# Eight instead of four column tiles of an MLP product by seven products, with a narrow first product

## The chip, the cores and the metric

The kernel runs on one core of one Trainium2 chip. The metric is device time in microseconds (us) of one execution. Three runs of the kernel before the change gave 1551.36, 1551.41 and 1552.81 us, median 1551.41. TensorE is called PE, VectorE DVE, ScalarE ACT; SP issues the loads.

## The reference

One decoder layer on 256 tokens with 2048 features: a mixer sub-layer (gated linear recurrence and windowed attention), then the MLP that the change touches, then a final RMSNorm. All operands are float32.

```python
h2 = _modulate(_rms_norm(x, norm2_g[l]), shift2, scale2)
ff = jnp.square(jax.nn.relu(jnp.einsum("bsd,df->bsf", h2, w_ff1[l])))
x = x + gate2[:, None, :] * jnp.einsum("bsf,fd->bsd", ff, w_ff2[l])
return _rms_norm(x, final_g)
```

`w_ff1` is 2048 x 8192, `w_ff2` 8192 x 2048. With tiles of 128, ff1 has 64 column tiles of 16 row tiles each, and ff2 16 column tiles of 64 row tiles.

## The kernel before

**Precision.** Each float32 operand is split into a rounded high part and the rest as a low part (`split` for activations, L165 to L167; for weights `w_round`, L178 on ACT, and `w_rest`, L183 on DVE). A product is high x high, high x low, low x high: three matmuls with 256 moving columns in the narrow form (`gemm`, L204 to L206), or one with 512 columns (high and low of the activations side by side) and one with 256 in the wide form (`gemm_wide`, L226 to L232). The wide form leaves two halves of a bank, which ACT copies (L236) and DVE adds (L237); where `join=False` the two halves are taken one after the other.

**Chunks.** The MLP runs in four chunks of 16 ff1 column tiles each. In a chunk, `ff1_unit(c, f)` computes one column tile of the first product (f from 0 to 15; called F below) and keeps its square; then `ff2_unit(c, f)` multiplies the 16 squares with the chunk's rows of one column tile of `w_ff2` and adds the result to the residual `x1[f]` on DVE (L1183). Each such unit reads 1 MB of weights.

**Seven products.** In chunks 1 to 3 the ff2 column tiles 0 to 3 are not computed one by one. A `sum_step` (called S below) takes two row tiles (p of 8 pairs) and four column tiles: as a 2 x 2 block product, with the token halves of the two squares against the four blocks of 128 x 256 weights, by Winograd's form of Strassen's scheme. It has seven block products instead of eight, each again three matmuls with 256 moving columns (L1017 to L1019), 21 in all, which add up over the eight steps in seven half banks. `token_sums` (L974 to L985) makes the four sums of the squares (L978 to L981 on DVE, L983 on ACT, L984 on DVE), `weight_sums` (L987 to L999) the four sums of the weights: it loads 2 x 256 KB in rows of 512 bytes (L991), L993 makes two differences, then one 1024-column part is rounded and split (L178, L183), L996 and L997 make the last two sums, and a 768-column part is rounded and split. At a chunk's end the seven results go out of PSUM to `yt` (L1025 on ACT in chunk 1, L1027 on DVE adding in chunks 2 and 3); after chunk 3 `join_sums` (L1038) combines them and `take_sums` turns them back with transposes (L1045) and adds them to `x1` (L1047).

**Order of the work.** `units` lists the units of the whole kernel. Before a unit runs, the weights of the two units after it are asked for (LOOK = 2). Loads go through four `raw` buffers of 1 MB, taken in turn, and rounded and split parts through four `wh` and four `wl` buffers, two of each per unit. Within this, the framework's scheduler orders each engine's instructions ahead of time by costs of its own; each engine then runs its list in that order. PSUM has two pools of four banks: `pg` for units, `pa` for the seven products and transposes. In chunks 1 to 3 an S stands after every second F, the last one after ff2's first unit.

Of the kernel before, what the change touches and what calls it, by code (L numbers as in the profile page):

```python
# [66 lines left out]
def hybrid_layer(ctx: ExitStack, tc: tile.TileContext, x, xt, wada, w_p, w_r, w_f, vec, lruw, relb,  # L67
# [932 lines left out]
    yt = scr[:, 0:7 * T].rearrange("p (a b) -> p a b", b=T)  # L1000

    def sum_step(c, p, u):
        def run(w):
            if p == 0:
                pq[0] = [bank([P, 2, T]) for _ in range(4)]
            hi, lo = ts.pop(p)
            fa, fb = ff[c, 2 * p], ff[c, 2 * p + 1]
# [4 lines left out]
            for n, ((xh, xl), i, o) in enumerate(prods):
# [3 lines left out]
                end = p == KT // 2 - 1 and (n % 2 == 1 or n == 6)  # L1016
                te.matmul(ps, lhsT=xh, rhs=wh[:, e], start=p == 0 and n % 2 == 0, stop=False)  # L1017
# [2 lines left out]
            if p == KT // 2 - 1:  # L1020
                for n in range(4):
                    m = min(2, 7 - 2 * n)
                    y, ps = yt[:, 2 * n:2 * n + m], pq[0][n][:, 0:m]
                    if c == SUMMED_FROM:
                        se.activation(y, ps, AF.Copy)  # L1025
                    else:
                        ve.tensor_tensor(out=y, in0=ps, in1=y, op=ALU.add)  # L1027
                if c == 3:
                    later(3.0, join_sums)
                    for f in range(0, SUMMED, 2):  # L1030
                        later(1.6, take_sums, f)
        add_unit(run, lambda: weight_sums(u, p), 1024)

    def join_sums():
        p1, p2, p3, p5, p7, p6, p4 = (yt[:, i] for i in range(7))
        for o, a, b, op in ((p6, p1, p6, ALU.add), (p2, p1, p2, ALU.add), (p7, p6, p7, ALU.add), (p3, p6, p3, ALU.add),
                            (p3, p3, p5, ALU.add), (p4, p7, p4, ALU.subtract), (p5, p7, p5, ALU.add)):
            ve.tensor_tensor(out=o, in0=a, in1=b, op=op)  # L1038

    def take_sums(f):  # L1040
        ca, cb = (yt[:, 2], yt[:, 3]) if f == 0 else (yt[:, 1], yt[:, 6])
        pt = bank([P, 2, T])
        for i in range(2):
            for b, y in enumerate((ca, cb)):
                te.transpose(pt[:, i, b * P:(b + 1) * P], y[:, i * P:(i + 1) * P], idt)  # L1045
# [165 lines left out]
    for f in range(16):  # L1211
        out_unit(f)
    for c in range(4):
        summed = SUMMED if c >= SUMMED_FROM else 0
        u2 = full[0] + 16
        for f in range(16):
            ff1_unit(c, f)
            if summed and f % 2 == 1 and f > 1:
# [133 lines left out]
```

## Time and profile before

| | |
|---|---|
| median of three runs | 1551.41 us |
| the profiled execution | 1553.18 us, its span 1551.4 us |
| PE busy | 1536.2 us, 99% |
| DVE busy | 1286.0 us, 83% |
| ACT busy | 932.7 us, 60% |
| chunk 1 | from 1010 us, ff2 from 1117 us |
| chunk 2 | from 1186 us, ff2 from 1293 us |
| chunk 3 | from 1362 us, ff2 from 1469 us, the end at 1551 us |

The span is the time from the first to the last instruction on the core. Views used: the page (busy times, the chain of waits that ended last), windows (busy times of each engine in a stretch), instructions of one line (their count, first and last start), and timelines: start, duration, engine, line, operation, output and inputs, count, and in brackets the engine's idle time before it with what ended it. A duration is longer by some 0.08 us than the distance from one start to the next, because DVE starts an instruction before the one ahead has quite ended; distances between starts are what add up.

### The profile page before, as it was taken

The numbers are of one execution on the slowest core, as the hardware profiler recorded it, in microseconds if no ns is written. First come the engines' busy times: TensorE is split into PE (matmuls) and PEld (weight loads), VectorE is DVE, ScalarE is ACT, GpSimd is POOL, SyncE is SP. The second block draws the span as 40 slices with busy tenths as digits, with TensorE's granted clock in tenths as the row PEclk, the third lists the DMA queues.
The fourth block names the chain that finished last, engine by engine and source line by source line (L and its number), as shares of the span: only waits on it lengthen the run. The fifth ranks groups of instructions, "written<-read, shape, count | busy, mean of one in ns | idle before, by whom it ended". The sixth has DMA issues, their size and how long they took to land.

```text
span 1551.4 us, 25653 instructions
## 1 busy us (share of the span) xinstructions
PE 1536.2 (99%) x10137; PEld 1394.9 (90%) x10137; DVE 1286.0 (83%) x2030; ACT 932.7 (60%) x1538; POOL 0.2 (0%) x4
## 2 busy tenths in 40 slices
PE   8999999999999999999999999999999999999998
PEld 7999999999988888888889988888988888888887
DVE  5899888889889899999898877888866887678885
ACT  5763456657998674444466763366744765357764
POOL 0000000000000000000000000000000000000000
PEclk9999999999999999999999999999999999999999
DMA  9899977564676759988877666865654556546551
GB/s 371 335 387 332 354 277 256 210 247 177 259 256 241 275 203 340 353 307 298 331 277 278 218 248 244 326 224 182 214 201 174 179 194 227 189 154 204 195 210 57
DMA packets 84744, 387.93 MB, mean 250 GB/s; under 512 B 7344, under 2 KB 36368, under 8 KB 44432
## 3 DMA queue, kind: packets, MB, share of 16 engines
q1 hardware_dynamic: 79632, 381.51, 67.4%
q10 hardware_dynamic: 4992, 4.79, 1.0%
q8 instruction: 79, 1.29, 0.3%
q14 instruction: 41, 0.34, 0.1%
HBM read 384.13 MB, written 2.15 MB: 249 GB/s over the span
## 4 chain that ended last, share of the span: by engine, by line
PE 95%; ACT 3%; DMA 1%; DVE 1%; issue 0%; SPq 0%; DVEq 0%; ACTq 0%
PE pg L230 41%; PE pg L229 20%; PE pg L204 6%; PE pg L205 6%; PE pg L206 6%; PE pg L232 1%; PE pa L1017 1%; PE pa L1019 1%; PE pa L1018 1%; PE pg L1066 1%; PE pg L1065 1%; PE pg L1064 1%; PE pg L370 1%; ACT wh L178 1%; DMA ra<-in_wada_dram 1%; PE pa L678 1%
## 5 line engine op out<-in xcount | busy, mean ns | idle before, releaser
L230 PE MATMUL pg<-k,wh 128*128 128x512 f32 x2832 | 981.6, 394 | 0.6 <-DVE k L167 0.6
L178 ACT ACTIVATE wh<-rw 128x1024 fp32r<-128x1024 f32 (+1 forms) x542 | 559.5, 1041 | 444.3 <-PE pg L230 297.9
L183 DVE TENSOR_TENSOR wl<-rw,wh 128x1024 fp32r<-128x1024 f32 (+1 forms) x542 | 643.8, 1200 | 157.9 <-ACT wh L178 152.3
L229 PE MATMUL pg<-k,wl 128*128 128x256 f32 x2655 | 743.5, 280 | 0.0
L230 PEld LDWEIGHTS pg<-k,wh 128*128 128x128 f32 x2832 | 521.4, 188 | 108.3 <-PE pg L230 0.9
L229 PEld LDWEIGHTS pg<-k,wl 128*128 128x128 f32 x2655 | 499.4, 188 | 8.3 <-ACT k L166 0.7
L204 PE MATMUL pg<-k,wh 128*128 128x256 f32 x878 | 249.3, 284 | 0.0
L205 PE MATMUL pg<-k,wh 128*128 128x256 f32 x878 | 245.4, 280 | 0.0
L206 PE MATMUL pg<-k,wl 128*128 128x256 f32 x878 | 245.1, 280 | 0.0
L283 DVE CUSTOM_DVE_ANT_0 ra<-ra,scr,vc 128x2048 f32<-128x2048 f32 x96 | 225.1, 2345 | 10.2 <-DMA ra<-in_wada_dram 7.8
L204 PEld LDWEIGHTS pg<-k,wh 128*128 128x128 f32 x878 | 165.0, 188 | 4.8 <-issue 4.6
L205 PEld LDWEIGHTS pg<-k,wh 128*128 128x128 f32 x878 | 165.0, 188 | 0.2
L206 PEld LDWEIGHTS pg<-k,wl 128*128 128x128 f32 x878 | 164.8, 188 | 0.0
L1183 DVE SCALAR_TENSOR_TENSOR k<-pg,mod,k 128x256 f32<-128x256 f32 x100 | 48.3, 483 | 18.6 <-PE pg L230 17.1
L236 ACT ACTIVATE t<-pg 128x256 f32<-128x256 f32 x127 | 46.6, 367 | 24.4 <-PE pg L230 24.4
L237 DVE TENSOR_TENSOR t<-pg,t 128x256 f32<-128x256 f32 x127 | 52.9, 417 | 2.9 <-ACT t L236 2.9
L232 PE MATMUL pg<-k,wl 128*128 128x256 f32 x177 | 49.4, 279 | 0.0
L686 ACT ACTIVATE t<-t,as 128x128 f32<-128x128 f32 x64 | 28.4, 445 | 22.3 <-DVE as L683 22.3
L1064 PE MATMUL pg<-z,wh 128*128 128x258 f32 x144 | 40.8, 284 | 0.0
L1065 PE MATMUL pg<-z,wh 128*128 128x256 f32 x144 | 40.8, 284 | 0.0
L1066 PE MATMUL pg<-z,wl 128*128 128x258 f32 x144 | 40.7, 283 | 0.0
L232 PEld LDWEIGHTS pg<-k,wl 128*128 128x128 f32 x177 | 33.2, 188 | 6.5
(217 smaller groups left out, 1354.5 us busy)
## 6 DMA issues: line engine op xcount, KB each, us to landing
rw<-in_w_f_dram SPq DMA_DIRECT2D x188, 1024.0 KB, 4.9
ra<-in_wada_dram SPq DMA_DIRECT2D x96, 1024.0 KB, 6.5
rw<-in_w_r_dram SPq DMA_DIRECT2D x30, 1024.0 KB, 5.0
rw<-in_w_p_dram SPq DMA_DIRECT2D x29, 960.0 KB, 7.0
rw<-in_w_f_dram SPq DMA_DIRECT2D x48, 256.0 KB, 3.5
bt<-ud ACTq DMA_DIRECT2D x8, 512.0 KB, 3.6
k<-in_w_p_dram SPq DMA_DIRECT2D x9, 256.0 KB, 11.3
lw<-in_lruw_dram SPq DMA_DIRECT2D x4, 512.0 KB, 5.7
```

The lines of the kernel that those rows point to most:

```text
L178: pin(se.activation(wh[:, :c], raw[:, o:o + c], AF.Copy))
L183: pin(ve.tensor_tensor(out=wl[:, :c], in0=raw[:, o:o + c], in1=wh[:, :c].bitcast(F32), op=ALU.subtract))
L204: pin(te.matmul(ps, lhsT=wh[:, w], rhs=hl[:, 0], start=k == 0, stop=False))
L205: pin(te.matmul(ps, lhsT=wh[:, w], rhs=hl[:, 1], start=False, stop=False))
L206: pin(te.matmul(ps, lhsT=wl[:, w], rhs=hl[:, 0], start=False, stop=k == n - 1))
L229: te.matmul(ps[:, 0], lhsT=wl[:, w], rhs=hl[:, 0], start=False, stop=False)
L230: te.matmul(ps, lhsT=wh[:, w], rhs=hl, start=k == 0, stop=k == n - 1)
L232: te.matmul(ps[:, 0], lhsT=wl[:, w], rhs=hl[:, 0], start=False, stop=False)
L283: pin(ve.tensor_tensor_reduce(out=raw, in0=raw, in1=scr, scale=1.0, scalar=vc[:, V_BADA + c:V_BADA + c + 1], op0=ALU.mult, op1=ALU.add, ac ...
L1064: te.matmul(ps, lhsT=wh[:, e], rhs=z[k][:, 0:258], start=k == 0, stop=False)
L1065: te.matmul(ps[:, 0:256], lhsT=wh[:, e], rhs=z[k][:, 258:514], start=False, stop=False)
L1066: te.matmul(ps, lhsT=wl[:, e], rhs=z[k][:, 0:258], start=False, stop=k == KT - 1)
```

## The change

`QUADS = 2`: in chunks 1 to 3 the column tiles 0 to 7 of ff2 go by seven products, as two quads of four. Each pair of row tiles p now has two steps, q = 0 and 1, with the same token sums and other weights. The 14 results need seven banks: the four of `pa` and three of `pg`. One `pg` bank is left for the units in between, so ff1 in chunks 1 to 3 and ff2's column tiles 8 to 11 use the narrow form in half a bank (`half_of`; two units share a bank, f below 4 has its own). ff1's result then goes to ACT's Relu straight from PSUM, and L236 and L237 fall away there. A step stands after every F from f = 3 on, and after ff2's units 8, 9 and 10. `yt` has seven tiles instead of a slice of one. At the end two joins and four takes are due instead of one and two.

```diff
-SUMMED, SUMMED_FROM = 4, 1
+SUMMED, SUMMED_FROM, QUADS = 4, 1, 2
@@ sums_out, sum_step
-    def sum_step(c, p, u):
+    def sums_out(c):
+        if not yt:
+            yt.extend(scr[:, i * 2 * T:(i + 1) * 2 * T].rearrange("p (a b) -> p a b", b=T) for i in range(4))
+            yt.extend(pair() for _ in range(7 * QUADS // 2 - 4))
+        for y, ps in zip(yt, pq.pop(0)):
+            if c == SUMMED_FROM:
+                se.activation(y, ps, AF.Copy)
+            else:
+                ve.tensor_tensor(out=y, in0=ps, in1=y, op=ALU.add)
+        if c == 3:
+            for q in range(QUADS):
+                later(1.2, join_sums, q)
+            for f in range(0, SUMMED * QUADS, 2):
+                later(1.2, take_sums, f)
+    def sum_step(c, p, u, q):
         def run(w):
-            if p == 0:
+            if p == 0 and q == 0:
                 pq[0] = [bank([P, 2, T]) for _ in range(4)]
-            hi, lo = ts.pop(p)
+                pq[0] += [pg.tile([P, 2, T], F32, tag="pg", name=nm("pg")) for _ in range(7 * QUADS // 2 - 4)]
+            hi, lo = ts[p]
...
-            for n, ((xh, xl), i, o) in enumerate(prods):
+            for n, ((xh, xl), i, o) in enumerate(prods, 7 * q):
@@ ff1_unit
-            gemm_wide(w, [zn[k] for k in range(KT)], out=t[:, 0])
-            se.activation(t[:, 0], t[:, 0], AF.Relu)
+            if c >= SUMMED_FROM:
+                se.activation(t[:, 0], gemm(w, 0, [zn[k] for k in range(KT)], half_of(f, f < 4)), AF.Relu)
+            else:
+                gemm_wide(w, [zn[k] for k in range(KT)], out=t[:, 0])
+                se.activation(t[:, 0], t[:, 0], AF.Relu)
@@ ff2_unit
+            if c >= SUMMED_FROM and f < SUMMED * QUADS + 4:
+                pss = [gemm(w, 0, acts, half_of(f))]
@@ the list of units
-        summed = SUMMED if c >= SUMMED_FROM else 0
+        summed = SUMMED * QUADS if c >= SUMMED_FROM else 0
+        steps = [(p, u2 + q * SUMMED, q) for p in range(KT // 2) for q in range(QUADS)] if summed else []
         for f in range(16):
             ff1_unit(c, f)
-            if summed and f % 2 == 1 and f > 1:
-                sum_step(c, f // 2 - 1, u2)
+            if f > 2 and steps:
+                sum_step(c, *steps.pop(0))
```

**DVE in ff1 of chunk 3.** Before: `wl` with 1024 columns from a raw that no L993 names is half of an F's weights (rw_14867, rw_14953), rw_14898 and rw_15044 are raws of two S steps. One S's second part (768 columns) and the next S's first difference (L993) stand in three F halves:

```order
L183 TENSOR_TENSOR wl_14871<-rw_14867,wh_14869 128x1024
L183 TENSOR_TENSOR wl_14875<-rw_14867,wh_14873 128x1024
L167 TENSOR_TENSOR k_14855<-t_14817,k_14855 128x256
L978 SCALAR_TENSOR_TENSOR t_14858<-t_14766,t_14817 128x128
L979 SCALAR_TENSOR_TENSOR t_14858<-t_14858,t_14766 128x128
L981 TENSOR_TENSOR t_14858<-t_14817,t_14858 128x128
L183 TENSOR_TENSOR wl_14904<-rw_14898,wh_14902 128x1024
L984 TENSOR_TENSOR ts_14864<-t_14858,ts_14863 128x512
L993 TENSOR_TENSOR rw_15044<-rw_15044 128x512
L183 TENSOR_TENSOR wl_14910<-rw_14898,wh_14908 128x768
```

There the raw for rw_15044 is the one that the F with rw_14867 gives back. Now, the same engine and stretch, from the last part of one S (rw_16025) to that of the next (rw_16125); F's raw is rw_16060, and the S after the next is rw_16233:

```order
L183 TENSOR_TENSOR wl_16037<-rw_16025,wh_16035 128x768
L984 TENSOR_TENSOR ts_16022<-t_16016,ts_16021 128x512
L996 TENSOR_TENSOR rw_16125<-rw_16125 128x256
L183 TENSOR_TENSOR wl_16064<-rw_16060,wh_16062 128x1024
L997 TENSOR_TENSOR rw_16125<-rw_16125 128x256
L993 TENSOR_TENSOR rw_16233<-rw_16233 128x512
L183 TENSOR_TENSOR wl_16068<-rw_16060,wh_16066 128x1024
L996 TENSOR_TENSOR rw_16233<-rw_16233 128x256
L183 TENSOR_TENSOR wl_16131<-rw_16125,wh_16129 128x1024
L167 TENSOR_TENSOR k_16122<-t_16070,k_16122 128x256
L183 TENSOR_TENSOR wl_16137<-rw_16125,wh_16135 128x768
```

With F and S in turn, the four raws make an S take over the raw of the S two before it: rw_16233 is loaded into the buffer of rw_16025, once the first row shown has read it. Five rows behind that row its first difference is due.

**The next step on DVE**, up to the last part of rw_16233; rw_16333 takes over the buffer of rw_16125, rw_16160 is the next F's:

```order
L997 TENSOR_TENSOR rw_16233<-rw_16233 128x256
L183 TENSOR_TENSOR wl_16164<-rw_16160,wh_16162 128x1024
L993 TENSOR_TENSOR rw_16333<-rw_16333 128x512
L183 TENSOR_TENSOR wl_16168<-rw_16160,wh_16166 128x1024
L978 SCALAR_TENSOR_TENSOR t_16224<-t_16070,t_16170 128x128
L980 TENSOR_TENSOR t_16224<-t_16070 128x128
L979 SCALAR_TENSOR_TENSOR t_16224<-t_16224,t_16070 128x128
L167 TENSOR_TENSOR k_16221<-t_16170,k_16221 128x256
L981 TENSOR_TENSOR t_16224<-t_16170,t_16224 128x128
L183 TENSOR_TENSOR wl_16239<-rw_16233,wh_16237 128x1024
L984 TENSOR_TENSOR ts_16230<-t_16224,ts_16229 128x512
L183 TENSOR_TENSOR wl_16245<-rw_16233,wh_16243 128x768
```

Here only two rows stand between L993 and the row that gives its buffer back, and the second half of the next F's weights (wl_16168) behind L993.

**PE near the end of chunk 3.** Before, the transposes of `take_sums` (L1045) stand inside an ff2 unit (pg_15665), more than one unit after the last S:

```order
L230 MATMUL pg_15665<-k_14508,wh_15536 128x512
L1045 MATMUL pa_15576<-idt,scr 128x128
L1045 MATMUL pa_15591<-idt,scr 128x128 x4
L229 MATMUL pg_15665<-k_14559,wl_15538 128x256
L230 MATMUL pg_15665<-k_14559,wh_15536 128x512
```

Now (L1056) half of them stand between ff2's units 11 and 12, one unit after the last S:

```order
L206 MATMUL pg_16890<-k_16637,wl_16888 128x256
L1056 MATMUL pa_16996<-idt,scr 128x128
L1056 MATMUL pa_17011<-idt,scr 128x128 x4
L1056 MATMUL pa_16996<-idt,scr 128x128 x3
L230 MATMUL pg_17129<-k_15174,wh_16946 128x512
```

What they turn comes from the joins on DVE (L1049), which stand there behind the weights of unit 12 (wl_16948, wl_16952) and three adds out of PSUM:

```order
L183 TENSOR_TENSOR wl_16948<-rw_16944,wh_16946 128x1024
L183 TENSOR_TENSOR wl_16952<-rw_16944,wh_16950 128x1024
L1010 TENSOR_TENSOR k_12765<-pg_15412,k_12765 128x512
L1010 TENSOR_TENSOR k_12766<-pg_15413,k_12766 128x512
L1010 TENSOR_TENSOR k_12767<-pg_15414,k_12767 128x512
L1049 TENSOR_TENSOR scr<-scr 128x256 x3
L1049 TENSOR_TENSOR k_12767<-scr,k_12767 128x256
L1049 TENSOR_TENSOR scr<-scr 128x256
```

The first join ends with the last row shown; the second has six more rows behind it, one of them after the first takes.

More of the change, by code (lines that the diff above doesn't have):

```diff
@@ L998, in weight_sums @@
         return parts + [w_rest(flat, 5 * T, 3 * T, w_round(flat, 5 * T, 3 * T))]
-    yt = scr[:, 0:7 * T].rearrange("p (a b) -> p a b", b=T)
-    def sum_step(c, p, u):
+    yt = []
+    def sums_out(c):
[13 more added lines that the diff above has]
+    def sum_step(c, p, u, q):
         def run(w):
-            if p == 0:
+            if p == 0 and q == 0:
                 pq[0] = [bank([P, 2, T]) for _ in range(4)]
-            hi, lo = ts.pop(p)
+                pq[0] += [pg.tile([P, 2, T], F32, tag="pg", name=nm("pg")) for _ in range(7 * QUADS // 2 - 4)]
+            hi, lo = ts[p]
             fa, fb = ff[c, 2 * p], ff[c, 2 * p + 1]
@@ L1015, in run @@
                 wh, wl = w[i]
-                end = p == KT // 2 - 1 and (n % 2 == 1 or n == 6)
+                end = p == KT // 2 - 1 and n % 2 == 1
                 te.matmul(ps, lhsT=xh, rhs=wh[:, e], start=p == 0 and n % 2 == 0, stop=False)
@@ L1019, in run, with joined, join_sums @@
                 te.matmul(ps, lhsT=xl, rhs=wh[:, e], start=False, stop=end)
[L1020 to L1031, printed above, removed]
+            if q == QUADS - 1:
+                ts.pop(p)
+                if p == KT // 2 - 1:
+                    sums_out(c)
         add_unit(run, lambda: weight_sums(u, p), 1024)
-    def join_sums():
-        p1, p2, p3, p5, p7, p6, p4 = (yt[:, i] for i in range(7))
+    def joined(q, i):
+        return yt[(7 * q + i) // 2][:, (7 * q + i) % 2]
+    def join_sums(q):
+        p1, p2, p3, p5, p7, p6, p4 = (joined(q, i) for i in range(7))
         for o, a, b, op in ((p6, p1, p6, ALU.add), (p2, p1, p2, ALU.add), (p7, p6, p7, ALU.add), (p3, p6, p3, ALU.add),
@@ L1040, in take_sums @@
     def take_sums(f):
-        ca, cb = (yt[:, 2], yt[:, 3]) if f == 0 else (yt[:, 1], yt[:, 6])
+        ca, cb = (joined(f // SUMMED, i) for i in ((2, 3) if f % SUMMED == 0 else (1, 6)))
         pt = bank([P, 2, T])
@@ L1056, in last_square, with half_of @@
         se.activation(x1[f], x1[f], AF.Copy, scale=vc[:, V_GF + f:V_GF + f + 1])
+    hb = [None]
+    def half_of(f, own=False):
+        if own or f % 2 == 0:
+            hb[0] = pg.tile([P, 2, T], F32, tag="pg", name=nm("pg"))
+        return hb[0][:, f % 2]
     def ff1_unit(c, f):
@@ L1180, in run @@
                 flush(5 * KT + f + 1)
-            ps = gemm_wide(w, [ff[c, j] for j in range(16)], join=False)
-            for i in range(2):
-                ve.scalar_tensor_tensor(out=x1[f], in0=ps[:, i], scalar=mod[:, 5 * KT + f:5 * KT + f + 1], in1=x1[f],
+            acts = [ff[c, j] for j in range(16)]
+            if c >= SUMMED_FROM and f < SUMMED * QUADS + 4:
+                pss = [gemm(w, 0, acts, half_of(f))]
+            else:
+                ps = gemm_wide(w, acts, join=False)
+                pss = [ps[:, 0], ps[:, 1]]
+            for ps in pss:
+                ve.scalar_tensor_tensor(out=x1[f], in0=ps, scalar=mod[:, 5 * KT + f:5 * KT + f + 1], in1=x1[f],
                                         op0=ALU.mult, op1=ALU.add)
@@ L1222, in hybrid_layer @@
             ff2_unit(c, f)
-            if summed and f == summed:
-                sum_step(c, KT // 2 - 1, u2)
+            if steps:
+                sum_step(c, *steps.pop(0))
     ready, credit, ada_credit = {0: split_w.pop(len(p_units))}, 0.0, 0.0
```

## The prediction

> **What bounds the kernel now.** F is an ff1 unit, S a step of the seven products, chunks are those of the MLP. I read the page first, then two windows, then the units.
>
> ```profile
> span 1551.4 us, 25653 instructions
> PE 1536.2 (99%) x10137; PEld 1394.9 (90%) x10137; DVE 1286.0 (83%) x2030; ACT 932.7 (60%) x1538; POOL 0.2 (0%) x4
> ...
> PE 95%; ACT 3%; DMA 1%; DVE 1%; issue 0%; SPq 0%; DVEq 0%; ACTq 0%
> ...
> core 0: us, PE busy (x) PEld busy (x) DVE busy (x) ACT busy (x) POOL busy (x), PEclk, DMA share, GB/s
> 1186.40:1293.10 106.70, 106.70 (x661) 95.62 (x660) 85.04 (x138) 72.17 (x114) 0.00 (x0) 1.00 0.54 183
> 1293.10:1362.40 69.30, 69.30 (x407) 61.26 (x406) 47.08 (x60) 29.21 (x31) 0.00 (x0) 1.00 0.57 205
> ```
>
> PE is busy throughout and is 95% of the chain that ended last; in chunk 2 (its ff1, then its ff2) it never stops, at a granted clock of 1.00. So the stream of matmuls is the time, as long as everything else keeps up. DVE is second, at 80% (85.04 of 106.7 us) in ff1, where the steps are. Its waits there matter for what follows:
>
> ```profile
> engine line waited for: us in total, times, longest us
> ACT wh L178 <- PE pg L230: 29.7, 30, 1.7
> DVE wl L183 <- ACT wh L178: 14.5, 19, 1.9
> DVE rw L993 <- DMA rw<-in_w_f_dram: 6.2, 6, 1.6
> ```
>
> This is chunk 2's ff1. ACT waits for PE to free weight buffers, DVE waits for ACT: both are ahead of PE. But DVE also waits six times for an S's load, while PE is not hurt.
>
> **PE's stream.** The units, from the first and last start of one matmul per unit, of one per row tile, and from a timeline:
>
> ```profile
> L232 PE MATMUL pg<-k,wl x15: 274/278/281, 1125.2 to 1203.4; 128*128 128x256 f32 x15
> ...
> L206 PE MATMUL pg<-k,wl x74: 274/278/283, 152.0 to 177.7; 128*128 128x256 f32 x74
> ...
> 1222.33 0.28 PE L1017 MATMUL pa<-wh,k 128*128 128x256 f32 x1
> ...
> 1224.81 0.40 PE L230 MATMUL pg<-k,wh 128*128 128x512 f32 x1
> ...
> 1483.90 0.71 PE L1045 MATMUL pa<-idt,scr 128*128 128x128 f32 x5
> ```
>
> A wide unit takes 78.2/14 = 5.586 us. L206 comes once per row tile in the narrow form, so a narrow unit is 16 x 25.7/73 = 5.633 us, 0.047 more. An S is 1224.81 - 1222.33 = 2.48 us. A transpose, with 0.27 us for the last one, is (0.71 - 0.27)/4 = 0.11 us.
> The change removes four wide units in each of three chunks, 12 x 5.586 = 67.0 us, and adds eight S in each, 24 x 2.48 = 59.5. It makes 48 F and 12 ff2 units narrow: 60 x 0.047 = 2.8 us. It adds eight transposes: 0.9. PE's stream changes by -67.0 + 59.5 + 2.8 + 0.9 = **-3.8 us**. That is all that can be won. The join of F that falls away (L236 on ACT, L237 on DVE) was hidden, and so are the fewer residual adds.
>
> **DVE and the load of an S.** Where F and S take turns, PE needs 5.633 + 2.48 = 8.11 us for a pair. DVE's rows in one cycle of before:
>
> ```profile
> 1211.48 2.35 DVE L183 TENSOR_TENSOR wl<-rw,wh 128x1024 fp32r<-128x1024 f32 x2
> 1213.75 0.42 DVE L167 TENSOR_TENSOR k<-t,k 128x256 fp32r<-128x256 f32 x1
> 1214.08 0.29 DVE L978 SCALAR_TENSOR_TENSOR t<-t,t 128x128 f32<-128x128 f32 x1
> 1214.40 0.29 DVE L979 SCALAR_TENSOR_TENSOR t<-t,t 128x128 f32<-128x128 f32 x1
> 1214.73 0.29 DVE L981 TENSOR_TENSOR t<-t,t 128x128 f32<-128x128 f32 x1
> 1215.26 1.23 DVE L183 TENSOR_TENSOR wl<-rw,wh 128x1024 fp32r<-128x1024 f32 x1 [0.24 <-ACT wh L178]
> 1216.40 0.69 DVE L984 TENSOR_TENSOR ts<-t,ts 128x512 fp32r<-128x512 f32 x1
> 1218.23 0.69 DVE L993 TENSOR_TENSOR rw<-rw 128x512 f32<-128x512 f32 x1 [1.15 <-DMA rw<-in_w_f_dram]
> 1218.84 0.95 DVE L183 TENSOR_TENSOR wl<-rw,wh 128x768 fp32r<-128x768 f32 x1
> 1219.71 0.42 DVE L237 TENSOR_TENSOR t<-pg,t 128x256 f32<-128x256 f32 x1
> 1220.05 0.41 DVE L996 TENSOR_TENSOR rw<-rw 128x256 f32<-128x256 f32 x1
> ...
> 1200.11 0.93 SPq L991 DMA_DIRECT2D rw<-in_w_f_dram  x2
> 1205.52 6.08 SPq L173 DMA_DIRECT2D rw<-in_w_f_dram  x2
> 1213.86 0.93 SPq L991 DMA_DIRECT2D rw<-in_w_f_dram  x2
> ...
> 1200.00 0.41 DVE L237 TENSOR_TENSOR t<-pg,t 128x256 f32<-128x256 f32 x1
> ...
> 1203.73 0.69 DVE L993 TENSOR_TENSOR rw<-rw 128x512 f32<-128x512 f32 x1
> ```
>
> From start to start: L183 with 1024 columns 1.14 us, with 768 0.87, L993 0.61, L984 0.60 (0.69 less the overlap), L996 or L167 0.34, the four small ones of the token sums 1.05 together. The rows below the first stretch give the **refill**: DVE gave the raw back at 1213.75, SP issued the S's load 0.1 us later, L993 ran at 1218.23, after 4.48 us, 1.15 of them with DVE idle. The two F loads had been issued by 1211.60 (1205.52 + 6.08), 2.3 us before. With no load in the 5.5 us before (issue at 1200.11) it took at most 3.73 us, from 1200.00 to 1203.73, for L993 did not wait.
> In the order after the change an S takes over the buffer of the S two before it, and its L993 stands three to five rows behind the row that gives that buffer back. DVE can't do anything else meanwhile: behind L993 stands the second half of the next F's weights. So a step on DVE, from one S's last part to the next one's, is refill plus the rows from L993 on. From the two stretches shown:
> first, 4.2 + L993 0.61 + L183 1.14 + L996 0.34 + L183 1.14 + L167 0.34 + L183 0.87 = 8.6 us;
> next, 4.2 + 0.61 + 1.14 + token sums 1.05 + L167 0.34 + 1.14 + L984 0.60 + 0.87 = 9.95 us.
> Counted so, the 13 steps from the first to the fourteenth S of a chunk are four of the first kind, three of about 10, four of 9.35 (no L984), and two of 7.2 (there both halves of F stand ahead of L993): 4 x 8.6 + 3 x 10.0 + 4 x 9.35 + 2 x 7.2 = 116.2 us. PE needs 13 x 8.11 = 105.4. DVE falls 10.8 us behind.
> What it is ahead at the start is little: F's second weight half can be rounded only when PE has left the F before (0.2 to wake, ACT's L178 1.06, L183 1.14: 2.4 us after), and PE needs it an S and half an F later, 2.48 + 2.8 + 0.2 = 5.5. So 3.1 us are covered, and from about the eighth F on PE waits: 10.8 - 3.1 = 7.7 us in a chunk. The three chunks have the same order: **+23 us**.
> The refill is the unknown. With 3.73 us, a chunk loses 13 x 0.47 = 6.1 less, 1.6 us, in all 5. With 4.48 it loses 3.6 more, 11.3, in all 34. I take 4.2: a load of F goes out shortly ahead of the first kind of step, as here, but half a pair, 4 us, ahead of the other, and two rows show 4.48 and at most 3.73.
> The Trainium skill, DMA: Bandwidth & Descriptors, section Anatomy of one DMA, puts a transfer at 2.0 us plus its bytes at 436 GB/s, for the other kind of queue. For 0.5 MB that is an estimate of 3.2 us; the rows above bound it at 3.73 with nothing else loading and show 4.48 with an F load ahead. By it a step would be 1.0 us shorter, 116.2/13 - 1.0 = 7.9 us, and DVE would keep up: the first rival.
>
> **The end of chunk 3.** Behind the last S, PE has one narrow unit, 5.63 us, until the first transposes. DVE has in that time two L183 (2.28), three adds out of PSUM and four rows of the first join, and before the second takes six more.
>
> ```profile
> 1479.99 1.61 DVE L1027 TENSOR_TENSOR scr<-pa,scr 128x512 f32<-128x512 f32 x3
> 1481.52 2.09 DVE L1038 TENSOR_TENSOR scr<-scr 128x256 f32<-128x256 f32 x6
> ```
>
> A row of a join is 0.34 us; of the three adds one has half the columns, so one with 512 is (1.53 - 0.34)/2 = 0.6. Up to the first join's end: 2.28 + 1.8 + 5 x 0.34 = 5.8; with the second 7.8, while PE gets there after 5.63 + 0.9 + 1.4 = 7.9. After this DVE has takes, square sums and unit 13's weights to do at once. I take **+1.5 us**, between 0 and 4. Evacuations at the ends of chunks 1 and 2 are covered by unit 11.
>
> **Sum.** -3.8 + 23 + 1.5 = +20.7. The profiled execution took 1553.18 us around a span of 1551.4 us, 1.8 above the median of the runs; the difference goes onto the median: 1551.4 + 20.7, rounded to 1572 us. Ends: -3.8 + 5 + 0 gives 1553, -3.8 + 34 + 4 gives 1586.
>
> **Rivals.**
> One: the refill is hidden, and PE's stream sets the time. The point from which it decides is a mean step of 8.11 + 3.1/13 = 8.35 us, a refill of 3.6. For it: 3.73 is an upper bound, L993 did not wait there. Against it: the wait at 1218.23 with F's load ahead, and that half of the steps have it so. Then -3.8 + 1 gives 1548.6 us. The Trainium skill, Perfetto Trace Analysis, Identifying the Most-Contended Engine, says to cut the engine with the highest occupancy first; that is PE, and by this rule the time falls with its stream, as here. The same page takes evenly repeated bubbles as a sign of too few buffers, which would be the forecast.
> Two: the bank of the narrow F is late. ACT does Relu behind the rounding that PE frees at F's end (1.06 us), so the bank is free about 0.2 + 1.06 + 0.4 = 1.7 us into an S of 2.48. If ACT is held up by more than 0.8 us, PE waits at every second unit. With 0.5 us at 21 of them: 10 us on top of the forecast, 1582. Against it: ACT's 60%.
> Three: the loop costs little, but the end costs more: joins and takes hold PE for 5 us, and 3.8 are won: 1553.
>
> **How the numbers follow.** Forecast 0.72, rival one 0.13, two 0.08, three 0.07. The range 1553 to 1586 holds the forecast's bounds, rival two and rival three's edge; it leaves out rival one and what both bounds miss. A difference of 0.2%, 3.1 us, is about what a measurement of this kernel can tell from no change. Slower by more: 0.80 (forecast, two, a little of three). Within: 0.13 (the rest of three, half of one). Faster by more: 0.07.
>
> **What would show it.** Right: in each ff1 of chunks 1 to 3 L993 waits for the load some 14 times, 1.3 to 2.8 us each, near 30 us in all instead of 6; PE idles for DVE's L183, ahead of a second weight half, from the eighth F on, 6 to 9 us per chunk; narrow F of 5.63 us and S of 2.48. Wrong: L993 waits under 1 us on average, PE without gaps in chunk 2, or PE waiting for ACT's Relu instead.

## The result, and the profile after

Five runs of the changed kernel gave 1567.38 to 1570.11 us, median **1568.42 us**; five of the kernel before, beside them, 1551.36 to 1554.05, median 1552.81. The ratio is **1.0104 (95% interval 1.0089 to 1.0119)**: 16 us slower. The prediction was 1572 us: 21 us slower, 23 of them for DVE's wait for an S's load, less what PE's stream would win. Direction and place were right; some terms were not.

The page of the profiled execution after the change: span, PE's busy row and the chain of work that ended last, by engine and by line.

```profile
span 1568.2 us, 28025 instructions
PE 1541.7 (98%) x11225; PEld 1444.7 (92%) x11225; DVE 1302.1 (83%) x2059; ACT 923.7 (59%) x1517; POOL 0.2 (0%) x4
...
PE 77%; DVE 9%; DMA 8%; ACT 3%; issue 2%; SPq 0%; DVEq 0%; ACTq 0%
PE pg L230 24%; PE pg L229 11%; PE pg L204 10%; PE pg L206 10%; PE pg L205 10%; DMA rw<-in_w_f_dram 7%; DVE wl L183 6%; ACT wh L178 1%; PE pg L1084 1%; PE pg L1083 1%; PE pg L1082 1%; DMA ra<-in_wada_dram 1%; PE pg L232 1%; PE pa L678 1%; PE pa L725 1%
```

The chain was 95% PE before. Now a sixth of it runs through DVE and DMA, and by line these are loads of the MLP's weights (7%) and L183 (6%). DVE is busy for the same 83%: it has not become a busier engine, it has become one that is waited for. Where, the waits of chunk 2 tell, from its first F into ff2's unit 8 (engine, line, what it waited for: us in all, times, longest):

```profile
DVE rw L993 <- DMA rw<-in_w_f_dram: 29.6, 14, 3.5
ACT wh L178 <- PE pg L205: 27.7, 20, 2.3
ACT ts L983 <- DVE t L981: 25.3, 7, 5.2
PEld pg L206 <- DVE wl L183: 5.0, 9, 1.3
DVE wl L183 <- ACT wh L178: 3.9, 5, 1.6
PE pg L206 <- DVE wl L183: 2.9, 4, 1.1
```

L993 waits 14 times for 29.6 us in all, where it was 6 times for 6.2 before. PE and its weight loads wait at L206, the matmul that needs F's rest part, for L183. One such place, DVE first, then PE's row:

```profile
1281.95 0.95 DVE L183 TENSOR_TENSOR wl<-rw,wh 128x768 fp32r<-128x768 f32 x1
1282.81 0.42 DVE L997 TENSOR_TENSOR rw<-rw 128x256 f32<-128x256 f32 x1
1283.15 1.22 DVE L183 TENSOR_TENSOR wl<-rw,wh 128x1024 fp32r<-128x1024 f32 x1
1287.89 0.69 DVE L993 TENSOR_TENSOR rw<-rw 128x512 f32<-128x512 f32 x1 [3.52 <-DMA rw<-in_w_f_dram]
1288.50 1.22 DVE L183 TENSOR_TENSOR wl<-rw,wh 128x1024 fp32r<-128x1024 f32 x1
...
1289.77 0.38 PE L206 MATMUL pg<-k,wl 128*128 128x256 f32 x1 [1.07 <-DVE wl L183]
```

The 768-column L183 gives the raw back at 1282.81. L993 of the S that takes it over runs at 1287.89, 5.08 us later, 3.52 of them with DVE idle. Behind it stands the second half of F's weights (1288.50), and PE starts again when that is done.

A second stall stands in each chunk where ff2's unit 9 begins, behind an S (DVE, then PE):

```profile
1327.90 1.22 DVE L183 TENSOR_TENSOR wl<-rw,wh 128x1024 fp32r<-128x1024 f32 x1
1329.03 0.42 DVE L997 TENSOR_TENSOR rw<-rw 128x256 f32<-128x256 f32 x1
1329.37 0.48 DVE L1209 SCALAR_TENSOR_TENSOR k<-pg,mod,k 128x256 f32<-128x256 f32 x1
...
1329.01 0.28 PE L1035 MATMUL pg<-wh,k 128*128 128x256 f32 x1
1329.99 0.36 PE L204 MATMUL pg<-k,wh 128*128 128x256 f32 x1 [0.70 <-DVE k L1209]
```

Unit 9 writes the other half of unit 8's bank and waits until unit 8 has been read; DVE gets to that add (L1209) late. PE starts 0.98 us after the last matmul of the S instead of 0.12: 0.86 us, three times 2.6.

### The profile page after: what moved, and what is told of

Its sections match the earlier page's. It is cut to its first block, busy times and chain, and to the rows that moved or that the text cites. A ratio compares the mean times of both kernels' runs of the same rounds, so it can differ in the third digit from the quotient of the medians.

```text
span 1568.2 us, 28025 instructions
## 1 busy us (share of the span) xinstructions
PE 1541.7 (98%) x11225; PEld 1444.7 (92%) x11225; DVE 1302.1 (83%) x2059; ACT 923.7 (59%) x1517; POOL 0.2 (0%) x4
## 4 chain that ended last, share of the span: by engine, by line
PE 77%; DVE 9%; DMA 8%; ACT 3%; issue 2%; SPq 0%; DVEq 0%; ACTq 0%
PE pg L230 24%; PE pg L229 11%; PE pg L204 10%; PE pg L206 10%; PE pg L205 10%; DMA rw<-in_w_f_dram 7%; DVE wl L183 6%; ACT wh L178 1%; PE pg L1084 1%; PE pg L1083 1%; PE pg L1082 1%; DMA ra<-in_wada_dram 1%; PE pg L232 1%; PE pa L678 1%; PE pa L725 1%
## 5 line engine op out<-in xcount | busy, mean ns | idle before, releaser
L178 ACT ACTIVATE wh<-rw 128x1024 fp32r<-128x1024 f32 (+2 forms) x566 | 575.8, 1029 | 404.4 <-PE pg L230 149.7
L183 DVE TENSOR_TENSOR wl<-rw,wh 128x1024 fp32r<-128x1024 f32 (+2 forms) x566 | 667.6, 1188 | 100.4 <-ACT wh L178 97.2
L230 PE MATMUL pg<-k,wh 128*128 128x512 f32 x1680 | 581.7, 394 | 0.7 <-DVE k L167 0.7
L206 PE MATMUL pg<-k,wl 128*128 128x256 f32 x1838 | 517.2, 282 | 10.1 <-DVE wl L183 9.5
L204 PE MATMUL pg<-k,wh 128*128 128x256 f32 x1838 | 518.9, 282 | 2.1 <-DVE k L1209 2.1
L205 PE MATMUL pg<-k,wh 128*128 128x256 f32 x1838 | 515.3, 280 | 0.0
L229 PE MATMUL pg<-k,wl 128*128 128x256 f32 x1575 | 441.7, 281 | 0.0
L230 PEld LDWEIGHTS pg<-k,wh 128*128 128x128 f32 x1680 | 308.9, 188 | 64.8 <-PE pg L230 0.9
L206 PEld LDWEIGHTS pg<-k,wl 128*128 128x128 f32 x1838 | 346.0, 188 | 14.7 <-DVE wl L183 14.4
L204 PEld LDWEIGHTS pg<-k,wh 128*128 128x128 f32 x1838 | 346.2, 188 | 7.4 <-issue 5.5
L205 PEld LDWEIGHTS pg<-k,wh 128*128 128x128 f32 x1838 | 345.8, 188 | 0.3
L229 PEld LDWEIGHTS pg<-k,wl 128*128 128x128 f32 x1575 | 296.1, 188 | 5.4 <-ACT k L166 0.8
L993 DVE TENSOR_TENSOR rw<-rw 128x512 f32<-128x512 f32 x48 | 33.2, 692 | 86.3 <-DMA rw<-in_w_f_dram 86.3
L983 ACT ACTIVATE ts<-t 128x512 fp32r<-128x512 f32 x24 | 15.2, 634 | 80.8 <-DVE t L981 80.8
L236 ACT ACTIVATE t<-pg 128x256 f32<-128x256 f32 x79 | 28.9, 366 | 24.4 <-PE pg L230 24.4
L686 ACT ACTIVATE t<-t,as 128x128 f32<-128x128 f32 x64 | 28.4, 445 | 22.4 <-DVE as L683 22.4
L1209 DVE SCALAR_TENSOR_TENSOR k<-pg,mod,k 128x256 f32<-128x256 f32 x64 | 30.8, 481 | 10.9 <-PE pg L230 7.6
L167 DVE TENSOR_TENSOR k<-t,k 128x256 fp32r<-128x256 f32 x80 | 33.5, 420 | 3.9 <-ACT k L166 3.9
## 6 DMA issues: line engine op xcount, KB each, us to landing
k<-in_w_p_dram SPq DMA_DIRECT2D x9, 256.0 KB, 10.8
```

The source lines that it names most:

```text
L167: pin(ve.tensor_tensor(out=hl[:, 1], in0=src, in1=hl[:, 0].bitcast(F32), op=ALU.subtract))
L178: pin(se.activation(wh[:, :c], raw[:, o:o + c], AF.Copy))
L183: pin(ve.tensor_tensor(out=wl[:, :c], in0=raw[:, o:o + c], in1=wh[:, :c].bitcast(F32), op=ALU.subtract))
L204: pin(te.matmul(ps, lhsT=wh[:, w], rhs=hl[:, 0], start=k == 0, stop=False))
L205: pin(te.matmul(ps, lhsT=wh[:, w], rhs=hl[:, 1], start=False, stop=False))
L206: pin(te.matmul(ps, lhsT=wl[:, w], rhs=hl[:, 0], start=False, stop=k == n - 1))
```

## The experiments

Each starts from the changed kernel unless it says otherwise. A "step" is the stretch on DVE from one S's last part to the next one's; the refill is the time from the row that gives a raw back to L993 of the S that takes it over.

**1. DVE's sums in the order of the program.**

```diff
-        ve.tensor_tensor(out=raw[:, 4:6], ...)
+        pin(ve.tensor_tensor(out=raw[:, 4:6], ...))
```
The same is done for L183 of an S, L996 and L997 (`pin` keeps the instructions given to it in the order in which the program issues them).

> The changed kernel with one thing altered: DVE's rows of an S's weight sums (L993, L183, L996, L997) keep the order of the program, so that the first difference of an S stands behind the last part of the S before it. The work is the same. Theory (the refill loop): in the changed kernel F waits 16 us in all (6.5, 6.2 and 3.4 us in the three chunks) because L993 waits in DVE's queue for a buffer that was given back only a few rows before; here the refill has a whole step of some 8 us to land in. L993's waits fall from 86 us to under 15, the F stalls go, time 1550 to 1555 us. Rival (DVE has simply too much to do between two S steps, whatever its order): the waits move to other rows, the time stays at 1565 us or more.

Measured 1593.01 us, 1.0262 (1.0245 to 1.0279) of the kernel before: 25 us slower than the changed kernel. The theory's time did not come; by the numbers this is the rival's side, over 1565 us and with the waits at other rows. Waits in chunk 2's ff1:

```profile
DVE wl L183 <- ACT wh L178: 28.2, 26, 1.6
ACT wh L178 <- DVE rw L997: 16.5, 11, 2.5
ACT wh L178 <- DVE rw L993: 15.0, 10, 1.7
```

Among the sixty largest waits of this kernel there is none of L993 for a load any more, so that part was as the theory has it. But ACT's rounding of an S needs L993 and L997 first, and DVE's L183 needs that rounding: with the sums placed late the two engines wait for each other in turn, and PE for both. In the changed kernel, where L993 and L997 stand early, ACT's rounding does not wait for either. So this run doesn't tell whether the refill loop made the 16 us; it tells that a place can be too late as well as too early. Nor does it make the rival right, that DVE has too much to do whatever its order: DVE is busy for 1307.5 us in run 7 and 1320.3 in run 11, against 1302.1 in the changed kernel, and neither has the 16 us.

**2. One load in rows of 4096 bytes.**

```diff
-        for k in range(2):
-            e = (2 * p + k) * P
-            nc.sync.dma_start(out=raw[:, 2 * k:2 * k + 2]..., in_=w_f[u:u + SUMMED, :, e:e + P]...)
+        nc.sync.dma_start(out=raw[:, 0:4]..., in_=w_f[u + p // 2, :, p % 2 * 4 * T:(p % 2 + 1) * 4 * T])
```
The weights of an S are laid out in memory to fit.

> The changed kernel with one thing altered: the weights of an S lie on the chip's memory so that its 512 KB come by one transfer in rows of 4096 bytes instead of two in rows of 512. DVE's order of rows is that of the changed kernel. Theory (the refill loop): a step is the refill plus 4.66 us of rows on average (8.86 less 4.2), PE needs 8.16, so the stalls of F end when the refill falls below some 3.7 us (8.16 + 3.5/13 - 4.66 = 3.77). If it falls to 3.4 the time is 1551 to 1556 us; each 0.1 us of refill that is left above costs 1.3 us per chunk; if rows of 4096 bytes land no sooner, 1568. Rival (too much work on DVE): the waits at L993 shrink, others grow, 1565 us or more even with a refill of 3.4.

Measured 1561.32 us, 1.0056 (1.0041 to 1.0071): 7 us better than the changed kernel, with the same rows of DVE in the same order. The refill did not reach 3.4. Over the 42 steps whose raw comes from an S, its mean is 4.00 us, against 4.21 in the changed kernel, and the 13 steps of a chunk take 112.8, 111.9 and 112.7 us instead of 116.7, 115.2 and 113.7. That is 8.1 us less on DVE for 7.1 us less in all: time follows the refill. The group of L993's waits (L991 here), first after the change, then with this load:

```profile
L993 DVE TENSOR_TENSOR rw<-rw 128x512 f32<-128x512 f32 x48 | 33.2, 692 | 86.3 <-DMA rw<-in_w_f_dram 86.3
```
```profile
DVE rw L991 <- DMA rw<-in_w_f_dram: 75.0, 45, 3.6
```

**3. Both.**

> Both alterations together. Theory (the refill loop): what either removes is the same 16 us, so together no more than the better of the two: 1550 to 1555 us, within 2 us of it. Rival (order and transfer are two separate costs): the gains add up, to less than 1545 us. A PE stream without F stalls is 1552.8 - 67.0 + 24 x 2.485 + 60 x 0.09 + 0.9 = 1551.7 us, and 0.85 us more per chunk where ff2's unit 9 waits.

Measured 1593.56 us, 1.0268 (1.0253 to 1.0283), the same as experiment 1, and neither the theory's 1550 to 1555 us nor the rival's 1545. A quicker load is worth nothing where nothing waits for the load. It says nothing more on the loop.

**4. The narrow form alone, on the kernel before.**

```diff
-            gemm_wide(w, [zn[k] for k in range(KT)], out=t[:, 0])
-            se.activation(t[:, 0], t[:, 0], AF.Relu)
+            if c >= SUMMED_FROM:
+                se.activation(t[:, 0], gemm(w, 0, [zn[k] for k in range(KT)], half_of(f, f < 4)), AF.Relu)
...
+            if c >= SUMMED_FROM and 8 <= f < 12:
+                pss = [gemm(w, 0, acts, half_of(f))]
```

> The kernel before, with the narrow form alone: ff1 of chunks 1 to 3 and ff2's column tiles 8 to 11 there go in half banks, four column tiles by seven products as before. Nothing of the loop is there, since an S stands after every second F. By the narrow unit of the changed kernel's trace (5.68 us against 5.587 of a wide one) +60 x 0.09 = 5.4 us, 1558 us. By the prediction's 5.633 us +2.8, 1555.6 us. Rival (a late bank of the narrow form is part of what the changed kernel lost): over 1562 us, with PE waiting for L209x's Relu.

Measured 1567.28 us, 1.0098 (1.0083 to 1.0113): as slow as the whole change, and by the numbers the rival's side. But PE does not wait for Relu. It waits inside the S for the token sums, in front of L1019, the third matmul of a product. The waits of PE and of its weight loads over the whole kernel, which are the same twelve stops, and one of them:

```profile
PEld pa L1019 <- DVE ts L984: 5.1, 12, 0.4
PE pa L1019 <- DVE ts L984: 2.7, 12, 0.2
...
1236.66 0.28 PE L1018 MATMUL pa<-wl,ts 128*128 128x256 f32 x1
1237.17 0.39 PE L1019 MATMUL pa<-wh,ts 128*128 128x256 f32 x1 [0.23 <-DVE ts L984]
```

L1019 starts 0.51 us after the matmul ahead of it instead of 0.12. In the order planned for this kernel six of the eight S of a chunk are cut in two with an F in between, and their halves that need `ts` come before L984 is through; three more such stops wait for ACT's rounding (L178). L984's wait does not occur on PE in the changed kernel. From its first matmul to the next unit's, an S takes 2.85 us here on average (both halves together), 2.49 in the kernel before: 8.7 us more over the 24. The narrow units take what they take in the changed kernel: F0 to F3 of chunk 2 run from 1191.03 to 1213.74, 5.68 us each, so 60 x 0.09 = 5.4 us. Together that is 14.1 of the 15.2 us. So most of it is a cost of that kernel's own order; the whole time gives no price of the narrow form, the rows do.

**5. All three rows of the weight sums on GpSimd.**

```diff
-        ve.tensor_tensor(out=raw[:, 4:6], ...)
+        nc.gpsimd.tensor_tensor(out=raw[:, 4:6], ...)
```
and the same for L996 and L997.

> The changed kernel with the three rows of an S's weight sums (L993, L996, L997) on GpSimd instead of DVE. The wait for the refill then stands in GpSimd's queue, where nothing else is; DVE's own rows are 1.3 us fewer per step, and no row of DVE waits for a load but an S's own split. Theory (the refill loop through DVE's order): F's stalls of 16 us go, PE's stream sets the time: 1550 to 1556 us, L206 no longer waits for L183. Rival (the refill delays the S itself, whoever waits for it): 1565 us or more, with PE waiting at L1033 for the S's weights. What speaks for a part of that: in the order with late sums S waited too (1593 us), because ACT's rounding came behind DVE's differences.

Measured **1551.89 us**, 1.0 (0.999 to 1.001). The stalls of F and that of unit 9 are gone. The loads are as they were; they are waited for in a queue that holds up nothing else. The rival falls: the S itself has time. DVE's 13 steps of a chunk take 108.4, 109.3 and 108.6 us there, 2.3 to 3.2 more than PE's 106.1, and PE still does not wait for L183: DVE's lead at the start covers that much.

**6. Only the first of them there.**

> The changed kernel with only the first of the three rows (L993) on GpSimd; L996 and L997 stay on DVE and wait there for L993's result. F's second half now stands ahead of the waiting row, but the step from one S's last part to the next one's holds refill, GpSimd's row (at least DVE's 0.61 us, an estimate), L996 0.34, L997 0.34, L183 1.14, L167 0.34, L183 0.87: 7.8 us after a refill of 4.2, and some 1 us more where the token sums stand between: 8.3 us on average against PE's 8.16. Theory (it is the length of this loop that counts, not which row waits): little falls behind in a chunk, 2 us, if GpSimd's row is as fast as DVE's, and 13 us more per chunk for each us that it is slower: 1553 to 1575 us, above the kernel with all three rows there. Rival (only F's second half behind L993 matters): the same time as with all three rows on GpSimd, within 2 us.

Measured 1577.31 us, 1.0158 (1.0143 to 1.0173). F's second half no longer stands behind the wait, yet the kernel is slower than the changed one:

```profile
DVE rw L996 <- POOL rw L993: 32.6, 13, 3.1
...
L993 POOL TENSOR_TENSOR rw<-rw 128x512 f32<-128x512 f32 x48 | 63.1, 1314 | 1453.3 <-DMA rw<-in_w_f_dram 1394.5 <-DVE k L1209 41.8 <-ACT wh L178 17.0
```

The first row is chunk 2's, the second the whole kernel's. L996 on DVE takes over the waiting, 13 times, and GpSimd's row takes 1.31 us where DVE's took 0.61 from start to start. With 0.7 us more the 8.3 us of the expectation become 9.0 per step, 117 us for 13; measured are 117.9, 115.6 and 117.4. PE now waits mainly inside the S, where L1034 needs the S's own L183 (14 times, 7.6 us of PE's idle time). So it is the loop's length and not F's place alone that counts. The time itself lies 2 us above the expected range: the 3 x 13 steps are 5.4 us longer than in the changed kernel, the kernel 8.9, and where the rest lies is open.

**7. A load in shorter rows, with another order.**

```diff
-            nc.sync.dma_start(out=raw[:, 2 * k:2 * k + 2]..., in_=w_f[u:u + SUMMED, :, e:e + P]...)
+            for h in (0, P // 2):
+                nc.sync.dma_start(out=raw[:, 2 * k:2 * k + 2]...[:, :, h:h + P // 2],
+                                  in_=w_f[u:u + SUMMED, :, e + h:e + h + P // 2]...)
```

> The changed kernel with an S's load in four transfers in rows of 256 bytes instead of two in rows of 512. The load can only be slower, the rows of DVE are the same; but the order of DVE's rows that is planned for it has L993 one to two rows later, behind the second half of F's weights. A step is then the refill plus 2.96 us of rows in the first kind (0.61 + 0.34 + 1.14 + 0.87) and some 3.4 in the second. Theory (refill plus the rows behind L993 in the order): with a refill of up to 4.9 us the step stays at PE's 8.16, the F stalls go although the load is slower: 1551 to 1558 us. Rival (the speed of the load alone sets the loss): slower than the changed kernel, 1570 us or more; each 0.1 us of refill costs 4 us in all.

Measured **1552.3 us**, 1.0001 (0.9991 to 1.001). A load in four pieces of 256-byte rows, and 16 us faster. Two steps of it (L994 is the first difference here, L997 and L998 the other sums):

```profile
1258.04 1.23 DVE L183 TENSOR_TENSOR wl<-rw,wh 128x1024 fp32r<-128x1024 f32 x1 [1.39 <-ACT wh L178]
1259.18 0.28 DVE L978 SCALAR_TENSOR_TENSOR t<-t,t 128x128 f32<-128x128 f32 x1
1260.33 0.69 DVE L994 TENSOR_TENSOR rw<-rw 128x512 f32<-128x512 f32 x1 [0.87 <-DMA rw<-in_w_f_dram]
...
1262.82 0.95 DVE L183 TENSOR_TENSOR wl<-rw,wh 128x768 fp32r<-128x768 f32 x1
...
1266.22 1.23 DVE L183 TENSOR_TENSOR wl<-rw,wh 128x1024 fp32r<-128x1024 f32 x1
1267.95 0.69 DVE L994 TENSOR_TENSOR rw<-rw 128x512 f32<-128x512 f32 x1 [0.51 <-DMA rw<-in_w_f_dram]
```

L994 now stands behind both halves of F (1258.04, 1266.22). From 1263.68, where the raw is given back, to 1267.95 it is 4.27 us, no quicker than before, but DVE fills them with rows that have to be done anyway. What this leaves of PE's stalls is seen in the first and last matmul that an S begins with, three chunks of the changed kernel, then of this one (L1033 and L1034 are the same line):

```profile
L1033 PE MATMUL pa<-wh,k x32: 273/281/287, 1031.4 to 1161.2; 128*128 128x256 f32 x32
L1033 PE MATMUL pa<-wh,k x32: 277/281/285, 1214.4 to 1343.9; 128*128 128x256 f32 x32
L1033 PE MATMUL pa<-wh,k x32: 276/282/290, 1397.0 to 1523.8; 128*128 128x256 f32 x32
```
```profile
L1034 PE MATMUL pa<-wh,k x32: 274/280/287, 1032.4 to 1154.7; 128*128 128x256 f32 x32
L1034 PE MATMUL pa<-wh,k x32: 276/281/285, 1207.9 to 1330.3; 128*128 128x256 f32 x32
L1034 PE MATMUL pa<-wh,k x32: 276/282/290, 1383.5 to 1505.8; 128*128 128x256 f32 x32
```

129.8, 129.5 and 126.8 us have become 122.3, 122.4 and 122.3: 7.5 + 7.1 + 4.5 = 19.1 us of stalls in the changed kernel, 2.6 of them in front of unit 9.

**8 and 9. F wide again, on top of 7 and of 5.**

```diff
-                se.activation(t[:, 0], gemm(w, 0, [zn[k] for k in range(KT)], half_of(f, f < 4)), AF.Relu)
+                se.activation(t, gemm_wide(w, [zn[k] for k in range(KT)], join=False), AF.Copy)
+                ve.tensor_tensor(out=t[:, 0], in0=t[:, 0], in1=t[:, 1], op=ALU.add)
+                se.activation(t[:, 0], t[:, 0], AF.Relu)
```

> The kernel with rows of 256 bytes (1552.3 us, PE without stalls in the three chunks), and F in chunks 1 to 3 wide again, in the one bank that is left: ACT copies both halves out at once (512 columns, an estimate of 0.6 us by L983's 0.64), DVE adds them in SBUF, and the next F finds the bank free if that copy ends within an S, 2.48 us. Theory (the narrow form costs PE 0.09 us per unit, 48 units 4.3 us, and nothing else): 1548 us. The bank is free 0.2 + 1.06 (L178 ahead on ACT) + 0.6 = 1.9 us into the S. Rival (one bank is too few for the wide form, the price of narrow is paid for a reason): PE waits for ACT's copy in front of F, 0.5 us or more at 39 places, 1565 us or more.

> The same wide F with the sums of an S on GpSimd (1551.9 us before this). In that trace DVE's rows beside GpSimd's are longer: L167 1.14 us on average against 0.42, L183 with 768 columns 1.24 against 0.95. Theory: 4.3 us less, 1547.6 us, since DVE still keeps up. Rival (DVE has no room left for a further row of 0.34 us per F while GpSimd holds it up): PE waits again for L183, 1553 us or more.

Measured 1548.54 us, 0.9972 (0.9962 to 0.9982), and 1549.09 us, 0.9978 (0.9969 to 0.9987). Both beat the kernel before. The 48 narrow units had cost 3.8 and 2.8 us, 0.06 to 0.08 each, against the 0.09 expected. One bank is enough for the wide form here. ACT clears it with one copy, and in run 8 PE waits for none of the 48:

```profile
L1100 ACT ACTIVATE t<-pg x48: 577/580/583, 1017.9 to 1479.8; 128x512 f32<-128x512 f32 x48
```

**10. Four transfers, but in rows of 1024 bytes.**

```diff
+        for s in range(4):
+            nc.sync.dma_start(out=raw[:, s], in_=w_f[u + p // 2, :, (p % 2 * 4 + s) * T:(p % 2 * 4 + s + 1) * T])
```

> An S's load in four transfers again, but in rows of 1024 bytes (the weights of an S laid out for it). It is at least as quick as two transfers in rows of 512, and quicker than the four in rows of 256 that took 1552.3 us. The order that is planned for it has L991 (the first difference) ahead of F's second half again. Counting the rows of its order (1.14, 0.87, 0.61, 0.34 and 0.22 us each) as refill plus what stands from the first difference to the last part of the S before it, the 13 steps of a chunk come to 112.5 us with a refill of 3.8, 115.1 with 4.0, 117.7 with 4.2; the same count gives 115.0 for the changed kernel (measured 113.7 to 116.7) and 112.4 for one transfer in rows of 4096 (measured 111.9 to 112.8); PE needs 106.1. Theory (refill plus the rows behind the first difference): 1560 to 1572 us, slower than the slow rows. Rival (the number of transfers, or a quicker load, is what helped): 1553 us or less.

Measured 1567.92 us, 1.01 (1.0084 to 1.0116), inside the theory's 1560 to 1572. The same number of transfers as in 7, and 15.6 us slower, with L993 (L991 here) in its early place:

```profile
DVE rw L991 <- DMA rw<-in_w_f_dram: 79.2, 47, 3.8
```

In 7 the same row waited 7.0 us in all. The page of either run has the same row for the load, 2.6 us from issue to landing:

```profile
rw<-in_w_f_dram SPq DMA_DIRECT2D x192, 128.0 KB, 2.6
```

The 13 steps of a chunk take 115.6, 113.4 and 116.0 us, at a mean refill of 3.97; the count of the expectation is 115.1 at 4.0. Neither the number of transfers nor their speed made 7 fast: the order did.

**11. Only the narrow F taken back.** The edit of 8, on the changed kernel with its own loads.

> The changed kernel with its loads as they are, and only the narrow F of chunks 1 to 3 taken back: F is wide in its one bank, ACT copies both halves out (0.58 us), DVE adds them. The order that is planned for it has the first difference behind F's halves; the same count as above gives 93.9 us for 13 steps at a refill of 4.2, far under PE's 13 x (5.59 + 2.48) = 104.9. Theory: no F stalls, and 48 narrow units fewer, 1548 to 1549 us, as with the rows of 256 bytes. Rival (the order of the two earlier kernels without stalls helped for another reason, their loads in four parts or the free DVE): 1555 us or more, L993 waiting 60 us or more.

Measured **1548.24 us**, 0.9976 (0.9966 to 0.9985): 0.24% faster than the kernel before, 20 us faster than the changed one. The order planned with F wide has an add more on DVE and a longer copy on ACT, and other places for L993. In each chunk, from the fifth S on, every second L993 runs a whole step after its raw was given back, behind both halves of an F, and does not wait. The others stand ahead of F's second half as before, but with some nine rows, about 4 us, in front of them instead of two to five. L993 waits 23.7 us in the whole kernel instead of 86.3:

```profile
DVE rw L993 <- DMA rw<-in_w_f_dram: 23.7, 23, 2.7
```

That the rows of DVE's order, counted with the durations of the kernel before, foretell this run, run 10 and run 7 is the strongest evidence for the loop. What changes the order changes other things with it in each of these runs; none moves L993 alone by one or two rows.

## Why the prediction was right, point by point

**The loop: right in place and kind.** "In each ff1 of chunks 1 to 3 L993 waits for the load some 14 times, 1.3 to 2.8 us each, near 30 us in all": 14 times, 29.6 us, up to 3.5. PE stops for L183 in front of a second weight half, first at F10, F8 and F9 in the three chunks ("from about the eighth F on"). Runs 5 and 7, where the wait stands elsewhere, lose none of it; run 2 shows that a quicker load in the same place helps by as much as it is quicker.

**The refill of 4.2 us: right in the mean, wrong by kind.** The mean over 42 steps is 4.21. But it is not one value: 24 of them lie between 3.68 and 4.0, the rest reach 5.5. The forecast took the first kind of step, in which it put F's load shortly ahead, for the slower one, and the trace shows the reverse. In the 12 steps of the first kind the refill is 3.91 us on average, and 11 of them lie between 3.7 and 3.95. In the 21 of the second kind (9.35 to 10 us in the forecast) it is 4.53, and 16 of them lie above 4.0. Twelve of these 21 had F's load (L173) going out 2.3 us ahead, as in the 4.48 of the kernel before, and all twelve lie above 4.0; in the first kind it went out 2.7 to 2.8 us ahead. The 5.08 us shown above is one of the twelve:

```profile
1280.25 0.34 SPq L173 DMA_DIRECT2D rw<-in_w_f_dram  x1
...
1282.92 0.92 SPq L991 DMA_DIRECT2D rw<-in_w_f_dram  x2
```

So a load of F shortly ahead goes with a slow refill, as the forecast had it, but in the other kind of step. It is not all: the twelve range from 4.03 to 5.51, and the nine others of the second kind, with F's load 3.5 to 3.9 us ahead, from 3.75 to 5.26. Why is open. That the mean came out at 4.2 all the same is luck. The estimate of 3.2 us by the Trainium skill (DMA: Bandwidth & Descriptors, Anatomy of one DMA) was not reached by any step; the shortest took 3.68.

**The 13 steps: 116.2 us foretold, 116.7, 115.2 and 113.7 measured.** PE's need was put at 13 x 8.11 = 105.4; with the S and the narrow unit as they ran it is 13 x 8.16 = 106.1. So DVE falls behind by 10.6, 9.1 and 7.6 us instead of 10.8. Of F's stalls, 7.5 + 7.1 + 4.5 less 2.6 for unit 9, 16.5 us are left (6.6, 6.2 and 3.6 by chunk; a part of them falls into ff2's unit 8), against **+23**: the largest miss. DVE falls less far behind, and its lead at the start covers 4.0, 2.9 and 4.0 us of it where 3.1 had been worked out: 106.1 + 3.1 would give stalls of 7.5, 6.0 and 4.5, 18 us.

**PE's stream: -3.8 us foretold, -1.1 by the rows as they ran.** The step that failed is the narrow unit. It was taken from the mixer, 5.633 us; in chunk 2's F0 to F3 (64 row tiles) it is between 16 x 22.3/63 = 5.66 and 16 x 22.4/63 = 5.69:

```profile
L206 PE MATMUL pg<-k,wl x64: 277/280/287, 1191.9 to 1214.2; 128*128 128x256 f32 x64
...
L204 PE MATMUL pg<-k,wh x64: 277/280/284, 1191.6 to 1214.0; 128*128 128x256 f32 x64
```

With 5.68, 60 x 0.09 = 5.4 us instead of 2.8: -67.0 + 59.6 + 5.4 + 0.9 = -1.1. Run 5 and run 7, without stalls, are at the time of the kernel before within 0.1%. So "all that can be won" was about a microsecond, and rival one would have ended near 1552, not 1548.6.

**Unit 9: not foreseen, 2.6 us.** "Evacuations at the ends of chunks 1 and 2 are covered by unit 11" left out the narrow units of ff2, which share a bank and are read by DVE. It is a consequence of the same delay: in runs 5 and 7 it is gone.

**The end of chunk 3: +1.5 foretold, about nothing.** The transposes begin 0.26 us after the last matmul of unit 11, where 0.12 is the usual distance:

```profile
1531.81 0.28 PE L206 MATMUL pg<-k,wl 128*128 128x256 f32 x1
1532.07 1.13 PE L1056 MATMUL pa<-idt,scr 128*128 128x128 f32 x8
```

**Sum as measured:** -1.1 + 16.5 + 2.6 = 18.0 us, and the spans differ by 16.8; chunk 1 began about 1 us earlier in this execution than in that of before. So the forecast is near for a reason and by luck: its term for DVE's wait was 6.5 us too large and that for the end 1.5, and the narrow units (2.7) and unit 9 (2.6), which it had too small or not at all, made up for two thirds of that. The rivals two and three did not come: L1099 is nowhere waited for by PE, and the end costs nothing.

**What was missed altogether** is how loosely the place of L993 hangs on the change. The prediction took the planned order as given, which was right for this kernel. That a load in four pieces of short rows, or an F that is wide, gets another order and with it the whole 16 us back could have been read from the plan of such a variant beforehand.

## What to carry to other kernels

Where a load waits for a buffer that an engine gives back, and a row of that same engine waits for the load, there is a loop: its period is the refill plus the rows from the waiting one to the one that gives back. Compare that period with the consumer's, not the engine's busy share (83% here, before and after): a row moved behind two others was worth 16 us, a load with rows eight times as long 7, and sums placed too late cost 25. Price a form of a unit from the place where it will run: the narrow unit was 0.04 us dearer there than where it was measured, which over 60 units was most of the gain.

## What was not expected of the hardware

DVE's rows get longer beside GpSimd's. In chunk 2's F and S of run 5, then of run 7 with no GpSimd:

```profile
L167 DVE TENSOR_TENSOR k<-t,k 128x256 fp32r<-128x256 f32 x15 | 17.2, 1148 | 0.1
L183 DVE TENSOR_TENSOR wl<-rw,wh 128x768 fp32r<-128x768 f32 x13 | 15.6, 1199 | 0.0
...
L993 POOL TENSOR_TENSOR rw<-rw 128x512 f32<-128x512 f32 x14 | 24.1, 1725 | 64.1 <-DMA rw<-in_w_f_dram 52.4 <-DVE t L979 8.3 <-DVE t L978 3.3
```
```profile
L183 DVE TENSOR_TENSOR wl<-rw,wh 128x768 fp32r<-128x768 f32 x13 | 12.4, 953 | 0.3 <-ACT wh L178 0.3
L167 DVE TENSOR_TENSOR k<-t,k 128x256 fp32r<-128x256 f32 x16 | 6.8, 423 | 0.5 <-ACT k L166 0.2
```

L167 takes 1.15 us instead of 0.42, and GpSimd's own L993 1.73 instead of the 1.31 of run 6. The Trainium skill, SBUF — State Buffer, section Who interferes with whom, says that a DVE instruction with two inputs in SBUF contends with a GpSimd instruction that reads SBUF, and that the shared pair of ports is an exclusive lock; L167 is of that kind, and the trace agrees. So DVE's busy share in run 5 (86% of the span) holds some of this lengthening.

Rows of 4096 bytes did not land an S's weights much sooner than rows of 512: of 42 refills 24 are between 3.65 and 3.95 us with two transfers in rows of 512, and 29 with one in rows of 4096; the mean moves from 4.21 to 4.00 by fewer slow ones. By the profile's pages a transfer of 256 KB in rows of 512 lands 3.2 us after its issue and one of 512 KB in rows of 4096 after 3.7 (medians), and SP needs 0.92 us to issue two: the single transfer saves an issue and lands later.
